# Second SwiGLU half step of a hybrid decoder layer: gate and up products by seven block products instead of eight

## The chip, the cores and the metric

The kernel runs on one core of a Trainium2 chip. Its engines are named as the profile names them: PE (matrix products, with PEld for the loads of its stationary operand), DVE (elementwise, VectorE), ACT (activations and copies, ScalarE), POOL (elementwise, GpSimd) and SP, which issues the DMAs. The metric is the device time of one execution in microseconds; a kernel is given by the median of its runs. Before the change it is 2705.25 us over 3 runs (2701.61 to 2705.65).

## The reference

One layer of a decoder trunk over 1056 tokens (1024 of a prompt, 32 sample tokens; 16 more tokens only in the first part), with D_MODEL 1024 and D_FF 2816, all in float32:

```python
def _swiglu(x, w_gate, w_up, w_down):
    return (jax.nn.silu(x @ w_gate) * (x @ w_up)) @ w_down

h = h + 0.5 * _swiglu(_rmsnorm(h, norm_ffn1), ffn1_w_gate, ffn1_w_up, ffn1_w_down)
z = _rmsnorm(h, norm_mix) @ w_in            # gated linear attention and S5 branches follow
merged = jax.nn.sigmoid(gate_a) * gla_out + jax.nn.sigmoid(gate_b) * s5_out
h = h + merged @ w_out
h = h + 0.5 * _swiglu(_rmsnorm(h, norm_ffn2), ffn2_w_gate, ffn2_w_up, ffn2_w_down)
return _rmsnorm(h, norm_final)
```

The change concerns the last three lines: the output projection, the second half step and the final norm.

## The kernel before

Activations lie transposed, features on the 128 partitions and tokens along the free axis, so a matrix with 1024 rows is 8 tiles of 128 by 1024. The 1056 tokens are cut in chunks `CH2` of 256, 384 and 416 columns. Each operand of a large product is held as two float32r parts, a rounded one and a rest (`xh`, `xl` of the activations, `wh`, `wl` of the weights), and each product is three matmuls: `wh` with `xh`, `wh` with `xl`, `wl` with `xh` (L702 to L704 in `group`). A job of 8 row tiles is 24 matmuls into one PSUM buffer of the pool `mm` (4 buffers).

The class `Weights` streams weight tiles of 128 x 1024 in the order of use: SP loads one (512 KB), ACT copies it to `wh` (L598), DVE subtracts to `wl` (L610), two tiles ahead of PE. `tiles` runs a list of jobs over the chunks; after each job `sch.slot()` lets background work go a step further. The program order of each engine is the order in which this code is written out; an engine executes its list in that order.

The output projection (`w_out`, from L1503) has 8 weight tiles and goes in two passes: 8 tiles over chunks 0 and 1, then the same 8 tiles over chunk 2. After each job DVE adds the PSUM to `h` (L36), ACT squares the result and POOL adds the square to a running sum (`nacc`, L36). When a chunk is complete, `sums` makes column sums on PE (L796) and a reciprocal root by 13 small DVE operations (`rq`); `apply` spreads it by PE (L814) and makes the normalized chunk: DVE multiplies from PSUM (`at`, L52), ACT rounds (`xh`, L692), DVE and POOL in turn subtract (`xl`, L693).

The second half step (`ffn`, L851) works through the 22 tiles of D_FF in groups of 2, 4, 4, 4, 4, 4. In a group each tile has a gate job and an up job for each chunk (72 matmuls each over the three chunks), then come the down jobs of the group, added to `h` by DVE (L52). The first group starts with three jobs on chunks 0 and 1, so that chunk 2 can be normalized beside them. The last group's down jobs go chunk by chunk, with the final norm behind each.

## Time and profile before

| what | value |
|---|---|
| median of 3 runs | 2705.25 us |
| profiled execution, own time | 2706.03 us |
| its span, first to last instruction | 2704.3 us |
| mean granted PE clock | 0.993 |
| busy PE / DVE / ACT / POOL | 98% / 46% / 26% / 18% |
| output projection, second pass | about 1894 to 1931 us |
| second half step, first gate job to last down job | about 1937 to 2693 us |

A line of the groups view gives the source line, engine, operation, output and inputs by their names, then the number of instructions, busy time and mean duration. Matmuls are pipelined: the duration of one (0.28 to 0.35 us) is longer than the distance from one start to the next, and it is the distance that counts. In a row of the timeline the first number is the start in us from the beginning of the span, the second the time from there to the end of the last of the merged instructions.

### The profile page before, as it was taken

How to read it: one execution, taken by the hardware profiler on the slowest of the kernel's cores; microseconds unless marked ns; L12 is line 12 of the kernel's file. 1: busy time of each engine (PE TensorE's matmuls, PEld its weight loads, DVE VectorE, ACT ScalarE, POOL GpSimd, SP SyncE). 2: the span in 40 equal slices, each digit the busy share in tenths (PEclk: the TensorE clock that was granted, in tenths of full speed). 3: DMA queues.
4: the chain of work that ended last, by engine and by line, in shares of the span. 5: the costliest groups of instructions: out<-in, count | busy, mean ns of one | idle time of the engine just before them, and what ended most of it. 6: DMA issues, size and time to landing. Idle time of an engine off the chain costs nothing. (4 is left out here: it accounts for less than half of the span.)

```text
span 2704.3 us, 41257 instructions
## 1 busy us (share of the span) xinstructions
PE 2654.9 (98%) x16796; PEld 2602.6 (96%) x16796; DVE 1237.9 (46%) x2677; ACT 713.8 (26%) x1303; POOL 479.1 (18%) x1006
## 2 busy tenths in 40 slices
...
GB/s 122 47 47 40 47 48 50 133 138 99 62 26 192 191 198 201 137 51 55 83 79 52 146 108 195 116 157 81 71 47 48 47 47 41 46 47 48 47 47 65
DMA packets 135790, 236.92 MB, mean 88 GB/s; under 512 B 21872, under 2 KB 100016, under 8 KB 134576
## 3 DMA queue, kind: packets, MB, share of 16 engines
...
## 5 line engine op out<-in xcount | busy, mean ns | idle before, releaser
L702 PE MATMUL mm<-xh,wh 128*128 128x256 f32 (+3 forms) x3648 | 1193.8, 327 | 19.6 <-ACT ta L1051 10.9
L704 PE MATMUL mm<-xh,wl 128*128 128x256 f32 (+3 forms) x3648 | 1186.3, 325 | 3.1 <-DVE wl L610 3.1
L703 PE MATMUL mm<-xl,wh 128*128 128x256 f32 (+3 forms) x3648 | 1184.1, 325 | 0.7 <-POOL xl L693 0.5
L702 PEld LDWEIGHTS mm<-xh,wh 128*128 128x128 f32 x3648 | 693.3, 190 | 30.6 <-ACT ta L1051 11.1
L704 PEld LDWEIGHTS mm<-xh,wl 128*128 128x128 f32 x3648 | 692.7, 190 | 8.9 <-DVE wl L610 4.0
L703 PEld LDWEIGHTS mm<-xl,wh 128*128 128x128 f32 x3648 | 693.3, 190 | 8.2 <-POOL xl L693 1.6
L610 DVE TENSOR_TENSOR wl<-wr,wh 128x1024 fp32r<-128x1024 f32 x218 | 270.4, 1240 | 347.4 <-ACT wh L598 346.7
L598 ACT ACTIVATE wh<-wr 128x1024 fp32r<-128x1024 f32 x218 | 229.0, 1052 | 483.8 <-PE mm L703 368.1
L702 PE MATMUL mm<-ah,wh 128*128 128x256 f32 (+3 forms) x1008 | 326.2, 324 | 0.6 <-DVE h L52 0.3
L703 PE MATMUL mm<-al,wh 128*128 128x256 f32 (+3 forms) x1008 | 326.3, 324 | 0.0
L704 PE MATMUL mm<-ah,wl 128*128 128x256 f32 (+3 forms) x1008 | 325.1, 323 | 0.0
L36 POOL TENSOR_TENSOR nacc<-nacc,nsq 128x384 f32<-128x384 f32 (+3 forms) x63 | 65.0, 1032 | 1049.0 <-ACT nsq L778 1044.7
L702 PEld LDWEIGHTS mm<-ah,wh 128*128 128x128 f32 x1008 | 189.4, 188 | 3.1 <-DVE h L52 0.7
L704 PEld LDWEIGHTS mm<-ah,wl 128*128 128x128 f32 x1008 | 189.5, 188 | 1.4
L703 PEld LDWEIGHTS mm<-al,wh 128*128 128x128 f32 x1008 | 189.3, 188 | 1.3
L692 ACT ACTIVATE ah<-at 128x256 fp32r<-128x256 f32 x132 | 66.1, 501 | 410.1 <-DVE at L36 410.1
L36 DVE TENSOR_TENSOR at<-mm,sg 128x256 f32<-128x256 f32 x132 | 69.3, 525 | 210.1 <-PE mm L704 199.2
L52 DVE SCALAR_TENSOR_TENSOR g<-mm,g 128x256 f32<-128x256 f32 (+2 forms) x144 | 74.5, 523 | 128.1 <-PE mm L704 127.6
L36 POOL TENSOR_TENSOR sg<-sg,root 128x384 f32<-128x384 f32 (+1 forms) x44 | 47.4, 1079 | 474.9 <-ACT sg L866 474.8
L52 DVE SCALAR_TENSOR_TENSOR h<-mm,h 128x256 f32<-128x256 f32 (+2 forms) x144 | 74.4, 526 | 74.0 <-PE mm L704 73.2
L693 DVE TENSOR_TENSOR al<-at,ah 128x256 fp32r<-128x256 f32 x132 | 70.4, 533 | 74.8 <-ACT ah L692 74.8
L49 POOL TENSOR_SCALAR rq<-rq,rq 128x1 f32<-128x1 f32 (+1 forms) x216 | 86.4, 400 | 21.7
...
## 6 DMA issues: line engine op xcount, KB each, us to landing
...
```

What stands on the lines that cost most here:

```text
L36: (eng or self.nc.vector).tensor_tensor(out=out, in0=a, in1=b, op=op)
L49: (eng or self.nc.vector).tensor_scalar(out=out, in0=a, scalar1=s1, scalar2=s2, op0=op0, **kw)
L52: self.nc.vector.scalar_tensor_tensor(out=out, in0=a, scalar=s, in1=b, op0=op0, op1=op1)
L598: self.nc.scalar.activation(out=h, in_=r, func=AF.Copy)
L610: e.tensor_tensor(out=l, in0=r, in1=h.bitcast(FT), op=OP.subtract)
L692: act.activation(out=xh, in_=t, func=AF.Copy)
L693: (eng or v).tensor_tensor(out=xl, in0=t, in1=xh.bitcast(FT), op=OP.subtract)
L702: pe.matmul(p, wh[:, b], xh, start=(k == 0), stop=False)
L703: pe.matmul(p, wh[:, b], xl, start=False, stop=False)
L704: pe.matmul(p, wl[:, b], xh, start=False, stop=(k == nk - 1))
```

## The change

Two adjacent tiles of D_FF, the two halves of the 1024 features and two halves of a block of tokens form a 2 x 2 by 2 x 2 block product. Before it was eight block products. Now it is seven, of sums and differences of blocks (Strassen's scheme in Winograd's form). One such set for gate or for up of two tiles is a `unit`: 7 products of 4 row tiles and 3 matmuls, 84 matmuls for each token block. There are two token blocks: block 0 with halves of 330 columns, block 1 with halves of 198. 11 pairs of tiles make 22 units.

- Sums of activations: seven operands a block, each in two float32r parts (`V[p][i]`), made once. For block 0 `early0` makes two of them beside the second pass of the output projection, and `late0` the other five beside the third. For block 1 `all1` makes them beside the first units: for each of 4 pairs of feature tiles, spread over 8 jobs, DVE makes 4 normalized blocks and 4 rests, POOL 4 differences and 3 rests, ACT 7 roundings.
- Sums of weights: the class `Stream` loads quarters of 128 x 512, makes four sums a unit on POOL, and rounds and subtracts each of seven on ACT and DVE (128 x 512 each), two products ahead (`LEAD = 2`).
- Outputs: three PSUM banks `a`, `b`, `c` a block; the order is `abcaaca`, so four products go into `a`. ACT copies partial sums out (`copy`), DVE adds them (`out`).
- The output projection has chunks of 264, 396 and 396 columns (`CHM`) and three passes, chunk 2, chunk 0, chunk 1, so 24 weight tiles instead of 16. `h` is one tile `H`, loaded after the projection before it.
- The first pairs (gate and up of pair 0, gate of pair 1, down of pair 0) run on block 0 alone and then on block 1 alone. From then on both blocks run within a product. The down jobs have widths 352 (or 330 and 396 for a single block), and the last two pairs go together, in four chunks of 330, 330, 198, 198 with the final norm behind each.
- Small edits elsewhere: scratch tiles shared in the S5 set-up, one load moved there, three instead of four buffers for the root.

```diff
+CHM = [(0, 264), (264, 396), (660, 396)]
...
+    HN, HP = (330, 198), (0, 660)
...
+    def nrm(p, k, i, R, t=None):
+        q0 = HP[p] + i * HN[p]
...
+        o.stt(t, H[:, k, q0:q0 + HN[p]], par[:, 24 + k:25 + k], R, OP.mult, OP.mult)
+        return t
+    def hi_(p, i, kp, t):
+        act.activation(out=V[p][i][0][:, kp], in_=t, func=AF.Copy)
+    def lo_(p, i, kp, t, eng):
+        xh, xl = V[p][i]
+        o.sub(xl[:, kp], t, xh[:, kp].bitcast(FT), eng)
...
+    def late0(R0, R):
+        roots(0, 1, R)
+        yield
+        x = {}
+        def a(kp):
+            x12, x22 = nrm(0, kp, 1, R), nrm(0, kp + 4, 1, R)
+            t1 = nrm(0, kp, 0, R0, tq.tile([P, HN[0]], FT, name="t1", bufs=2))
+            o.sub(t1, x12, t1)
+            hi_(0, IT1, kp, t1)
+            hi_(0, I22, kp, x22)
+            o.sub(x12, x22, x12, g)
+            x[kp] = [x12, x22, t1]
+        def b(kp):
+            x12, x22, t1 = x[kp]
+            lo_(0, IT1, kp, t1, v)
+            lo_(0, I22, kp, x22, v)
+            o.sub(x22, x22, t1)
+            hi_(0, IT3, kp, x12)
+            hi_(0, IT2, kp, x22)
+            t4 = nrm(0, kp + 4, 0, R0, tq.tile([P, HN[0]], FT, name="t4", bufs=2))
+            o.sub(t4, t4, x22, g)
+            x[kp].append(t4)
+        def c(kp):
+            x12, x22, t1, t4 = x.pop(kp)
+            lo_(0, IT3, kp, x12, g)
+            lo_(0, IT2, kp, x22, v)
+            hi_(0, IT4, kp, t4)
+            lo_(0, IT4, kp, t4, g)
+        for s in range(6):
+            for d, f in enumerate((c, b, a)):
+                kp = s - 2 + d
+                if 0 <= kp < 4:
+                    f(kp)
+            yield
+    def all1(R):
...
+    AB, A_, B_ = (0, 1), (0,), (1,)
+    plan = [(k, n, ps_) for ps_ in (A_, B_) for k, n in (("g", 0), ("u", 0), ("g", 1), ("d", 0))]
+    for n in range(1, NP - 1):
+        plan += [("u", n, AB), ("g", n + 1, AB)] + ([("d", n, AB)] if n < NP - 2 else [])
+    plan += [("u", NP - 1, AB), ("e", NP - 2, AB)]
...
+    class Stream:
+        LEAD = 2
...
+            T.append(((x, 0), lambda: a11, ()))
+            T.append((None, s3, ()))
+            T.append(((x, 1), lambda: a12, ()))
+            T.append((None, lambda: (o.add(a21, a21, a22, g), o.sub(a11, a22, r[0], g)), ()))
+            T.append(((x, 2), lambda: a21, (2,)))
+            T.append(((x, 3), lambda: a11, ()))
+            T.append((None, lambda: o.sub(a12, a12, a11, g), ()))
+            T.append(((x, 4), lambda: r[0], (0,)))
+            T.append(((x, 5), lambda: a12, (1,)))
+            T.append(((x, 6), lambda: a22, (3,)))
...
-    for m in range(8):
-        for c in range(2):
-            w_out(m, c, wi + m)
-    n3.fin(0, 1)
-    n3.fin(1, 3)
     for m in range(8):
         w_out(m, 2, wi + 8 + m)
-    n3.fin(2, 3)
...
+    sch.later(1, lambda: n3.sums(2))
+    sch.later(2, lambda: sch.add(early0(R0)))
     for m in range(8):
+        w_out(m, 0, wi + 8 + m)
...
+    sch.later(1, lambda: n3.sums(0))
+    sch.later(2, lambda: sch.add(late0(R0, SGs[0][:, 0])))
+    for m in range(8):
+        w_out(m, 1, wi + 16 + m)
+        if m == 6:
+            ws = Stream()
+    n3.sums(1)
+    sch.drain()
...
+    ws.advance(0)
+    ws.flush()
...
+    BANK = "abcaaca"
...
+        for i in range(7):
+            b = ws.get((x, i), num[0])
...
+            for p in ps_:
...
+                ps = bank[p, BANK[i]]
+                xh, xl = V[p][i]
+                for k in range(4):
+                    wh, wl = b[:, P * k:P * k + P], b[:, 512 + P * k:512 + P * k + P]
+                    pe.matmul(ps, wh, xh[:, k], start=FIRST[i] and k == 0, stop=False, skip_group_check=True)
+                    pe.matmul(ps, wh, xl[:, k], start=False, stop=False, skip_group_check=True)
+                    pe.matmul(ps, wl, xh[:, k], start=False, stop=(k == 3), skip_group_check=True)
```

DVE in the last pass of the output projection, from one addition to `h` (L36, out of `mm`) to the next; first before, then after. In both, `wl` is the rest of the next weights; after, `e1`, `e3`, `e5` are rests of operands and `t`, `t1`, `t4` normalized blocks or their sums.

```order
L36 TENSOR_TENSOR g2_18499<-mm_19252,g2_18499 128x416
L52 SCALAR_TENSOR_TENSOR at_19282<-g1_16624,par_65,sm_19227 128x384
L52 SCALAR_TENSOR_TENSOR at_19286<-g1_16624,par_65,sm_19227 128x384
L693 TENSOR_TENSOR xl1_19232<-at_19282,xh1_19231 128x384
L52 SCALAR_TENSOR_TENSOR at_19290<-g1_16624,par_65,sm_19227 128x384
L52 SCALAR_TENSOR_TENSOR at_19294<-g1_16624,par_65,sm_19227 128x384
L693 TENSOR_TENSOR xl1_19232<-at_19290,xh1_19231 128x384
L610 TENSOR_TENSOR wl_19301<-wr_19196,wh_19300 128x1024
L36 TENSOR_TENSOR g2_18499<-mm_19305,g2_18499 128x416
```

```order
L36 TENSOR_TENSOR h2_18493<-mm_19320,h2_18493 128x396
L36 TENSOR_TENSOR e3_19120<-t_19257,e2_19119 128x330
L36 TENSOR_TENSOR e1_19118<-t1_19311,e0_19117 128x330
L36 TENSOR_TENSOR e5_19122<-t_19309,e4_19121 128x330
L36 TENSOR_TENSOR t_19309<-t_19309,t1_19311 128x330
L52 SCALAR_TENSOR_TENSOR t4_19358<-h2_18493,par_65,r0_18783 128x330
L52 SCALAR_TENSOR_TENSOR t_19361<-h2_18493,par_65,xh0_19115 128x330
L52 SCALAR_TENSOR_TENSOR t_19363<-h2_18493,par_65,xh0_19115 128x330
L52 SCALAR_TENSOR_TENSOR t1_19365<-h2_18493,par_65,r0_18783 128x330
L36 TENSOR_TENSOR t1_19365<-t_19361,t1_19365 128x330
L617 TENSOR_TENSOR wl_19372<-wr_19268,wh_19371 128x1024
L36 TENSOR_TENSOR h2_18493<-mm_19374,h2_18493 128x396
```

Between the two additions six operations on 384 columns became nine on 330, and the root that the multiplications read is no longer in PSUM (`sm`) but in SBUF (`r0`, `xh0`).

POOL in the same pass, first before and then after, to the end of the pass and the first weight sum (`s3`). `nacc` and `f0` are the running sums of squares, `xl1`, `e7`, `e8` rests of operands.

```order
L36 TENSOR_TENSOR nacc0_19042<-nacc0_19042,nsq_19225 128x416
L693 TENSOR_TENSOR xl1_19232<-at_19243,xh1_19231 128x384
L693 TENSOR_TENSOR xl1_19232<-at_19286,xh1_19231 128x384
L693 TENSOR_TENSOR xl1_19232<-at_19294,xh1_19231 128x384
L36 TENSOR_TENSOR nacc0_19042<-nacc0_19042,nsq_19280 128x416
```

```order
L36 TENSOR_TENSOR f0_19158<-f0_19158,f2_18506 128x396
L36 TENSOR_TENSOR e7_19124<-t_19361,e6_19123 128x330
L36 TENSOR_TENSOR e8_19125<-t4_19412,xl0_19116 128x330
L36 TENSOR_TENSOR t4_19462<-t4_19462,t_19417 128x330
L36 TENSOR_TENSOR f0_19158<-f0_19158,f2_18506 128x396
L36 TENSOR_TENSOR e7_19124<-t_19415,e6_19123 128x330
L36 TENSOR_TENSOR e8_19125<-t4_19462,xl0_19116 128x330
L36 TENSOR_TENSOR f0_19158<-f0_19158,f2_18506 128x396
L36 TENSOR_TENSOR s3_19544<-wr_19465,wr_19466 128x512
```

The last sum of squares now stands behind the last operands of block 0, and the first weight sum behind that.

PE at the end of the last pass, before and after: the last matmul of the output projection and what follows.

```order
L704 MATMUL mm_19375<-xh2_17623,wl_19301 128x416
L702 MATMUL mm_19410<-xh0_19102,wh_19335 128x256
L703 MATMUL mm_19410<-xl0_19103,wh_19335 128x256
L704 MATMUL mm_19410<-xh0_19102,wl_19336 128x256
L702 MATMUL mm_19410<-xh0_19102,wh_19335 128x256
```

```order
L715 MATMUL mm_19471<-xh1_17614,wl_19372 128x396
L809 MATMUL sm_19504<-one1_68,f0_19158 128x1 x4
L1890 MATMUL mm_19542<-xh2_18781,wv_19534 128x330
L1891 MATMUL mm_19542<-xh2_18781,wv_19534 128x330
L1892 MATMUL mm_19542<-xh2_18781,wv_19534 128x330
```

Before, a gate job on a chunk that was long normalized followed at once; now the column sums of the chunk just finished stand in front of the first product.

## Rows read from the trace of the kernel before

**Rows 1.** The page, busy time of PE and its loads, share, instructions.
```profile
PE 2654.9 (98%) x16796; PEld 2602.6 (96%) x16796; DVE 1237.9 (46%) x2677; ACT 713.8 (26%) x1303; POOL 479.1 (18%) x1006
```
**Rows 2.** Windows: length, then busy PE, PEld, DVE, ACT, POOL, granted clock, DMA.
```profile
1993.57:2086.10 92.53, 92.53 (x578) 92.19 (x576) 21.82 (x31) 18.69 (x31) 0.00 (x0) 1.00 0.14 46
2086.10:2131.98 45.88, 45.88 (x289) 45.72 (x288) 17.64 (x29) 4.68 (x5) 0.00 (x0) 1.00 0.14 47
...
1916.30:1920.30 4.00, 4.00 (x13) 3.87 (x14) 2.25 (x3) 1.50 (x2) 1.94 (x2) 0.57 0.37 131
```
**Rows 3.** Timeline of PE, gate and up jobs, 256 and then 384 columns.
```profile
2051.40 0.28 PE L702 MATMUL mm<-xh,wh 128*128 128x256 f32 x1
...
2052.95 0.28 PE L703 MATMUL mm<-xl,wh 128*128 128x256 f32 x1
...
2055.31 0.33 PE L702 MATMUL mm<-xh,wh 128*128 128x384 f32 x1
...
2056.35 0.33 PE L702 MATMUL mm<-xh,wh 128*128 128x384 f32 x1
```
**Rows 4.** Timeline of PEld around the one-column sums of squares.
```profile
1894.49 0.53 PEld L796 LDWEIGHTS sm<-one,nacc 128*128 128x128 f32 x4
1894.94 0.19 PEld L702 LDWEIGHTS mm<-xh,wh 128*128 128x128 f32 x1
```
**Rows 5.** Timeline of PE, second pass of the output projection; in brackets idle time and releaser.
```profile
1913.67 0.35 PE L704 MATMUL mm<-xh,wl 128*128 128x416 f32 x1
1915.02 0.45 PE L702 MATMUL mm<-xh,wh 128*128 128x416 f32 x1 [1.00 <-ACT wh L598]
1915.32 0.35 PE L703 MATMUL mm<-xl,wh 128*128 128x416 f32 x1
1916.28 0.45 PE L704 MATMUL mm<-xh,wl 128*128 128x416 f32 x1 [0.61 <-DVE wl L610]
```
**Rows 6.** Groups by form from 1600 us on, DVE and POOL on SBUF operands.
```profile
L610 DVE TENSOR_TENSOR wl<-wr,wh 128x1024 fp32r<-128x1024 f32 x98 | 120.4, 1228 | 245.3 <-ACT wh L598 245.3
...
L693 DVE TENSOR_TENSOR al<-at,ah 128x384 fp32r<-128x384 f32 x22 | 12.3, 559 | 13.0 <-ACT ah L692 13.0
...
L693 DVE TENSOR_TENSOR al<-at,ah 128x256 fp32r<-128x256 f32 x22 | 9.4, 426 | 10.6 <-ACT ah L692 10.6
...
L36 POOL TENSOR_TENSOR nacc<-nacc,nsq 128x384 f32<-128x384 f32 x14 | 14.2, 1016 | 35.0 <-ACT nsq L778 35.0
L36 POOL TENSOR_TENSOR nacc<-nacc,nsq 128x256 f32<-128x256 f32 x7 | 5.2, 737 | 273.5 <-ACT nsq L778 273.5
```
**Rows 7.** Timeline of POOL, then of DVE, second pass of the output projection.
```profile
1905.73 1.02 POOL L693 TENSOR_TENSOR xl<-at,xh 128x384 fp32r<-128x384 f32 x1 [3.56 <-ACT xh L692]
1906.70 1.09 POOL L36 TENSOR_TENSOR nacc<-nacc,nsq 128x416 f32<-128x416 f32 x1
...
1915.06 2.11 POOL L36 TENSOR_TENSOR nacc<-nacc,nsq 128x416 f32<-128x416 f32 x1
...
1906.83 1.38 DVE L693 TENSOR_TENSOR xl<-at,xh 128x384 fp32r<-128x384 f32 x1
1908.13 1.21 DVE L610 TENSOR_TENSOR wl<-wr,wh 128x1024 fp32r<-128x1024 f32 x1
1909.27 0.58 DVE L36 TENSOR_TENSOR g<-mm,g 128x416 f32<-128x416 f32 x1
...
1915.00 1.23 DVE L610 TENSOR_TENSOR wl<-wr,wh 128x1024 fp32r<-128x1024 f32 x1 [0.91 <-ACT wh L598]
1916.14 0.58 DVE L36 TENSOR_TENSOR g<-mm,g 128x416 f32<-128x416 f32 x1
```
**Rows 8.** Waits of PE from 1600 us on: total, times, longest.
```profile
PE sm L814 <- DVE rq L52: 2.5, 1, 2.5
```
**Rows 9.** Groups by form from 1600 us on, ACT reading PSUM.
```profile
L862 ACT ACTIVATE sg<-mm 128x384 f32<-128x384 f32 x22 | 10.8, 490 | 80.9 <-PE mm L704 80.9
...
L862 ACT ACTIVATE sg<-mm 128x256 f32<-128x256 f32 x22 | 8.4, 384 | 23.3 <-PE mm L704 23.3
```

More of the change, by code (lines that the diff above doesn't have):

```diff
@@ L593, in split_to @@
     def split_to(self, n):
-        while self.ns <= min(n, len(self.order) - 1):
+        while self.ns <= min(n, self.end - 1):
             self.load_to(self.ns)
@@ new lines, in build, with roots @@
+    sqs = e_(2, 1, FT)
+    n3 = Norm(tp, CHM, h, 24, acc=lambda c, i: e_((1, 0, 0)[c], int(c != 2), FT), sq=sq_)
+    V = {}
+    I11, I21, IT1, IT2, IT3, I22, IT4 = range(7)
+    def roots(p, i, out):
+        q0, n = HP[p] + i * HN[p], HN[p]
+        r = ps_sm()[:, :n]
+        x = 0
+        while x < n:
+            c = max((c for c in range(3) if COLS[c] <= q0 + x), key=lambda c: COLS[c])
+            t = q0 + x - COLS[c]
+            cuts, rs = n3.rs[c]
+            j = max(j for j, u in enumerate(cuts) if u <= t)
+            a = t - cuts[j]
+            w = min(P - a, n - x)
+            pe.matmul(r[:, x:x + w], rs[:, j:j + 1].to_broadcast([P, P]), ident[:, a:a + w], start=True, stop=True)
+            x += w
+        act.activation(out=out, in_=r, func=AF.Copy)
@@ new lines, in build @@
+    pairs, i0 = [], A["order"][-n_ffn]
+    for gi, fs in enumerate(FGROUPS):
+        for a in range(0, len(fs), 2):
+            pairs.append((gi, a, i0 + 2 * a, i0 + 2 * len(fs)))
+        i0 += 3 * len(fs)
+    NP = len(pairs)
+    AB, A_, B_ = (0, 1), (0,), (1,)
[3 more added lines that the diff above has]
+    plan += [("u", NP - 1, AB), ("e", NP - 2, AB)]
@@ L1507, in w_out @@
         sch.slot()
+    TB = 8
+    ctq = ExitStack()
+    tq = pool(ctq, "f2q", side="right")
     for m in range(8):
[L1509 to L1518 removed]
+        w_out(m, 2, wi + m)
+    xf = {f"x{i}2": xa.tile([P, 2 * 1320 + 792], FR, name=f"x{i}2") for i in "hl"}
@@ new lines, in build @@
+    x0 = xa.tile([P, 4 * HN[0] + 4 * HN[1]], FR, name="xl0")
+    for j, i in enumerate((IT1, IT2, I22, IT3)):
+        V[0][i] = tuple(q4(e_(2 * j + q, 0)) for q in range(2))
+    V[0][IT4] = part(x0, 0, 0), q4(e_(8, 0))
+    sch.later(1, lambda: n3.sums(0))
[6 more added lines that the diff above has]
+    sch.drain()
+    wi += 24
+    ctq.close()
+    wctx.close()
@@ new lines, in build, with tt_, rest, a_home @@
+    fw = pool(ch2, "f2w")
+    fa = pool(ch2, "f2a")
+    ws.advance(0)
+    ws.flush()
+    num = [0]
+    BANK = "abcaaca"
+    FIRST = (True, True, True, False, False, False, False)
+    aH, lq, parity = {}, [], [0]
+    def tt_(p):
+        return tp.tile([P, HN[0]], FT, name="t", bufs=TB)[:, :HN[p]]
+    def rest():
+        for l, t, hh in lq:
+            o.sub(l, t, hh.bitcast(FT))
+        del lq[:]
+    def a_home(n, p, f, i):
+        if n == NP - 1:
+            return [V[p][I11][z][:, 2 * f + i] for z in range(2)]
+        q = HP[p] + HN[p] * i
+        return [aH[n][f][z][:, q:q + HN[p]] for z in range(2)]
@@ new lines, in cols, with down @@
+    def cols(n, t0, nn):
+        return [[y[:, t0:t0 + nn] for y in aH[n][f]] for f in range(2)]
+    def down(x, n, ps_):
+        rest()
+        for q in range(4):
+            b = ws.get((x, q), num[0])
+            num[0] += 1
+            for j in range(2):
+                m = 2 * q + j
+                for t0, nn in CHD[ps_]:
+                    ps = down_group([b], j, t0, nn, [cols(n, t0, nn)])
+                    o.stt(H[:, m, t0:t0 + nn], ps, 0.5, H[:, m, t0:t0 + nn], OP.mult, OP.add)
+                    ws.flush()
+                    sch.slot()
```

313 lines of the change are left out of this document (277 added, 36 removed).

## The prediction, made before the result was known

> **What bounds the kernel now.** I read the page's busy shares first: PE is busy for 98% of the span [rows 1]. A pipelined engine can look busy without being full, so next came the windows of one group of the second half step: 576 gate and up matmuls in 92.53 us, 288 down matmuls in 45.88 us, the granted clock 1.00, POOL idle, DVE busy for a quarter of it [rows 2]. That is 0.1606 and 0.1593 us a matmul. In the timeline the start-to-start distance is 1.55/13 = 0.119 us at 256 columns and 1.04/6 = 0.173 us at 384 [rows 3], so a matmul costs about 0.4 ns a column plus a fixed part. PE is full here; only fewer or shorter matmuls can save time, and every wait put in front of PE is lost in full. The place where DVE and POOL are late already is the second pass of the output projection [rows 5].
>
> **The change part by part.** The sum is made against the profiled execution, 2706.0 us (span 2704.3), 0.8 us above the median of 2705.25.
>
> *Gate and up.* Before: 22 tiles x 144 = 3168 matmuls x 0.1606 = 508.9 us. After: 22 units x 84 = 1848 at 330 columns and 1848 at 198. For 330 the line between the two distances gives 0.150 us. 198 columns is narrower than any matmul of this kind in the trace. Lower bound: the same line further down, 0.119 - 58 x 0.42 ns = 0.095. Upper bound: no shorter than at 256, 0.120. A third row is nearer than either: four loads of a full 128 x 128 stationary tile, with matmuls of one column between them, start 0.45/4 = 0.112 us apart [rows 4]. Each of our matmuls needs its own load, so the load is the floor. I take 0.112. After: 1848 x (0.150 + 0.112) = 484.2, that is -24.7 us (-56 at 0.095, -10 at 0.120).
> The Trainium skill, "TensorE: Matmul & The Clock Gate", section "LDWEIGHTS (loading the stationary operand)", puts a load at the number of its columns divided by 1.2 GHz, 107 ns for 128. The trace's 112 ns agrees within 5; by the page's figure the sum would be some 10 us lower (2040 narrow matmuls).
>
> *Down.* A pair of tiles takes 144 matmuls, 22.9 us. Nine pairs keep 1056 columns in other widths: 0.06 us more each, +0.5. The last two take 96 x (2 x 0.150 + 2 x 0.112) = 50.3 instead of 45.9: +4.4. Together +5. The stream of PE so saves 20 us.
>
> *Output projection.* The same number of matmuls over 264 + 396 + 396 columns: no change. Eight more weight tiles (1.2 us of DVE each) lie beside groups of 3 to 4.3 us: nothing, where DVE is free. It is not free in the third pass.
>
> *Operands beside the third pass.* What DVE and POOL do there must be added up together, since the trace shows that they do not run together on SBUF operands. POOL's `nacc` started at 1906.70 and ran 1.09 us; DVE's `xl`, started at 1906.83, took 1.38 us instead of the 0.56 of its like, to the end of POOL's operation and 0.4 us more. Conversely `nacc`, started at 1915.06 behind DVE's `wl` (1915.00, 1.23 us), took 2.11 us. DVE's addition out of PSUM at 1916.14 ran at its 0.58 us beside POOL [rows 6, 7]. So DVE operations with two SBUF inputs and POOL operations make one queue, and nearly all that `late0` adds is of these kinds: the root too is now in SBUF.
> The Trainium skill, "SBUF — State Buffer", section "Who interferes with whom", says the same: the port pair that DVE and GpSimd share is an exclusive lock, and the later one blocks fully. By that rule the operands cost what I add up now; without it they would fit beside PE, a rival below. The rows above agree with it.
> Prices, less the 0.08 (DVE) or 0.05 us (POOL) by which neighbours overlap [rows 6, 7]: at 330 columns DVE 0.42, POOL 0.85; `wl` 1.14; a `nacc` of 396 columns 1.0. From the end of the pass's third group five groups remain, 5 x 24 x 0.178 (396 columns on the same line) = 21.4 us. In that time stand 4 x 9 DVE operations (15.1), 4 x 4 POOL operations (13.6), 3 `wl` (3.4), 6 `nacc` (6): 38 us, 17 more than there is. Behind the queue's last piece, the last `nacc`, come the column sums, the root chain (PE waited 2.5 us for it at the end of before [rows 8]) and the rest of the first new weights (512 columns, 0.6): 3.4 more. PE's first product stands behind all of this. A walk through the queues in program order, with ACT's copies of the weights for the groups 7 and 8 standing behind the copies of operands, gives 26 us. Between 20 and 26 I take 23, in part ahead of the last two groups. Had the two engines run side by side, DVE alone would need 21.4 us and the end chain would leave 5.5: the lower bound.
> After a wait of some 2 us in the second pass of before, the clock fell to its lower level (1.2 GHz): 13 matmuls in 4 us at a mean granted clock of 0.57 [rows 2, 5]; that cost 1.6 us. I count 2 after the wait. Before's own waits there, 1.2 + 0.8 + 1.6 = 3.5, go. Sum: +21.5.
>
> *First units, one block at a time.* A unit on block 0 alone takes PE 84 x 0.150 = 12.6 us. In it the shared queue holds seven rests of weights (512 columns, 0.60: 4.2), four weight sums on POOL (2.2 ns a column from 256 to 384, so 1.25: 5.0) and 7/8 of a step of `all1` (8 DVE operations of 0.285, 7 on POOL of 0.56, at 198 columns: 5.4): 14.6; for up also 7 of 0.42: 17.5. Three units: 46.7 against 37.9 of PE. +9. On block 1 alone: 9.2 and 11.2 against 84 x 0.112 = 9.4: +2. In these units product 5 goes into bank `a` directly behind product 4, whose copy by ACT (0.33 to 0.44 us [rows 9]) it waits for, with the drain 0.5 to 0.6: six times, of which the three on block 0 lie within the 9. +2.
>
> *Units on both blocks.* The queue needs 4.2 + 5.0 + 7 x 0.705 = 14.1 us for up, PE 22.0; weights have two products of 3.1 us. Hidden. If the cover were gone, each microsecond missing would come 19 times.
>
> *The rest.* The set-up edits and the load moved lie beside full PE: nothing. `H` is now loaded after the gating projection; its first 1.6 MB must land within the first group's 4.3 us and four PSUM buffers behind it: nothing, up to 5. The end has a last chunk of 198 instead of 256 columns: -0.5.
>
> Sum: -20 + 21.5 + 9 + 2 + 2 - 0.5 = +14, from 2706.0 to 2720; less 0.8, on the footing of the median, 2719. I take 2720.
>
> **The rivals.** *A: the narrow matmul follows its columns* (0.095). For it: the line of rows 3 has no break down to 256. Against it: rows 4. PE saves 54 instead of 20; the units on block 1 then are bound by the shared queue (8.0 against 9.2 and 11.2), +3. 2720 - 31 = 2689, faster.
> The Trainium skill, "TensorE: Matmul & The Clock Gate", section "Back-to-back issue gap", gives a lone matmul columns over 2.4 GHz plus 2.5 ns, 85 ns here, which would take off 20 more; it names the load as a second limit, as rows 4 show it.
> *B: operands hidden as the schedule means it.* For it: DVE and POOL are busy for 46 and 18% of the span [rows 1]. Against it: rows 7. Then 5.5 + 2 - 3.5 = 4 for the passage and nothing for the units on block 0: -20 + 4 + 2 + 2 - 0.5 = -13, 2692, faster.
> *C: half of the queueing lies in slack that my walk misses* (POOL's pieces fall beside DVE's PSUM reads and its waits for ACT): 11 instead of 23, 4 instead of 9, so 2703, no change.
> *D: both go badly:* 0.120 a narrow matmul (+16), 28 at the passage (+5), 14 for the units on block 0 (+5), 5 for `H`: 2750. It decides where the load needs the fixed part of rows 3 on top.
>
> **How the numbers follow.** Forecast 2708 to 2740, chance 0.46; D and beyond 0.15; C 0.13; A 0.13; B 0.13. Times within 0.2% (5.4 us) are what a measurement of this kernel cannot tell from no change. Slower: 0.46 + 0.15 and a little of C: 0.62. Same: 0.12. Faster: 0.26. The range 2691 to 2746 leaves out about 0.1 on each side; the likeliest case alone has 2708 to 2740.
>
> **What would show it.** Right: PE starts at 198 columns 0.11 us apart; a wait of PE of 15 us or more in all in the last two groups of the output projection and before the first product, its releasers DVE `wl`, ACT `wh`, DVE `rq` and POOL's sum of squares; DVE operations there stretched beside POOL; a unit on both blocks at 22 us without waits. Wrong: narrow matmuls at 0.10 us or below, a passage under 8 us, or repeated waits for weights in the later units, which I priced at nothing.

## The result, and the profile after

The changed kernel takes 2754.47 us (median of 4 runs, 2753.86 to 2758.39); before takes 2705.45 (2701.61 to 2706.53). The ratio is 1.0187, 95% interval 1.0175 to 1.0199: slower by 49 us, where 14 were forecast, and outside the range of 2691 to 2746. The profiled execution took 2753.9 us (span 2752.1 against 2704.3, +47.8).

First the busy line of the page and then the stages of the second half step as windows of after. Columns: the stretch and its length, busy PE, PEld, DVE, ACT, POOL, then the granted clock, DMA share, GB/s. In order: the three passes of the output projection (the last with the wait for its column sums), the sums with the first product, the rest of the units on block 0, the units on block 1, two units on both blocks, and a projection down. The column sums of a pass stand behind the first group of the next one, so a window of a pass ends with that group.

```profile
PE 2666.3 (97%) x17434; PEld 2609.2 (95%) x17434; DVE 1465.8 (53%) x3187; ACT 848.4 (31%) x1688; POOL 649.4 (24%) x1149
```

```profile
1824.34:1867.10 42.76, 39.45 (x218) 38.72 (x217) 16.52 (x20) 13.47 (x18) 7.27 (x7) 0.96 0.59 200
1867.10:1902.38 35.28, 29.63 (x208) 27.91 (x206) 21.95 (x41) 15.05 (x25) 8.41 (x11) 0.95 0.34 109
1902.38:1951.60 49.22, 35.63 (x183) 34.11 (x183) 35.74 (x63) 18.56 (x37) 24.75 (x24) 0.86 0.21 73
1951.60:1961.54 9.94, 7.38 (x30) 6.96 (x31) 5.17 (x16) 1.41 (x3) 5.69 (x4) 0.51 0.09 26
1961.54:2010.10 48.56, 40.72 (x243) 38.01 (x242) 34.20 (x56) 25.19 (x57) 22.42 (x24) 0.96 0.19 60
2025.75:2067.44 41.69, 35.69 (x254) 33.55 (x253) 23.39 (x41) 18.16 (x41) 17.11 (x12) 0.88 0.23 73
2076.10:2120.42 44.32, 44.32 (x337) 44.32 (x337) 23.06 (x44) 18.06 (x41) 10.10 (x7) 1.00 0.17 54
2120.42:2143.53 23.11, 23.11 (x146) 23.11 (x145) 14.10 (x27) 2.75 (x5) 5.38 (x4) 1.00 0.12 35
```

Against [rows 1] PE is busy for as large a share and for 11 us longer, so its share tells nothing of the loss; DVE has 228 us more, POOL 170. The last two windows answer to [rows 2] and are close to what was forecast: two units take 44.32 us without a wait, 22.16 each, where 22.0 were forecast. The new stalls all lie in the 252 us ahead of them. (In PE's timeline of before, the second pass of the output projection lies at 1880 to 1922 us and the first gate job starts at 1922; the table ahead of the prediction has these times 9 to 15 us too late.)

The seven largest groups of waits of PE in after, from 1700 us on: total, times, longest. They answer to [rows 5, 8].

```profile
PE sm L809 <- POOL f L36: 9.8, 2, 9.2
PE mm L713 <- ACT wh L605: 8.1, 4, 3.7
PE mm L1892 <- DVE wv L36: 7.8, 9, 2.6
PE mm L1890 <- ACT t L1879: 5.3, 6, 2.2
PE mm L715 <- DVE wl L617: 4.6, 7, 1.2
PE mm L1890 <- ACT wv L1768: 3.1, 4, 1.1
PE sm L827 <- DVE rq L52: 2.5, 1, 2.5
```

The last stood in before as well; the others are spread over six releasers, and no single wait is the cause. The waits in the 252 us come to 39 us, which is less than the loss counted below: for the rest of it PE is busy, but slower. The granted clock of the six windows with stalls is 0.51 to 0.96, lowest in the window of the first product, behind the wait of 9.2 us.

For the account, each stage of after is set beside its matmuls at the full-clock distances that the timeline shows (198 columns 0.112 us, 264 0.122, 330 0.152, 396 0.180) plus its column sums and root broadcasts (0.11 us each or less). The other columns are runs below. Lengths in us, from the first matmul of a stage to that of the next:

| stage | matmuls alone | after | e1 | e2 | e3 | e6 | e7 | e12 | e8 | e11 |
|---|---|---|---|---|---|---|---|---|---|---|
| first pass | 37.5 | 42.8 | 43.5 | 43.5 | 42.5 | 37.5 | 42.4 | 44.1 | 37.5 | 37.5 |
| second pass | 26.3 | 35.3 | 26.8 | 36.6 | 28.8 | 35.3 | 35.3 | 35.3 | 27.9 | 28.1 |
| third pass, wait for its sums | 31.8 | 49.2 | 34.7 | 50.6 | 50.8 | 49.3 | 49.2 | 44.7 | 45.8 | 51.3 |
| sums, first product, roots | 3.7 | 9.9 | 10.1 | 9.2 | 9.1 | 10.1 | 9.8 | 9.1 | 9.5 | 4.7 |
| units on block 0 | 36.5 | 48.6 | 40.6 | 43.0 | 47.2 | 48.4 | 42.4 | 47.1 | 40.4 | 35.4 |
| down, block 0 | 14.6 | 15.7 | 14.5 | 17.0 | 15.7 | 15.7 | 16.1 | 15.7 | 19.6 | 18.0 |
| units on block 1 | 28.2 | 41.7 | 37.9 | 33.3 | 40.6 | 40.0 | 34.2 | 39.2 | 33.5 | 34.7 |

(e8 and e11 have blocks of other widths: there the matmuls alone are 29.3 us for the fifth row, 11.7 for the sixth and 30.7 for the last. In e11 the sums stand behind the first two products, which so count in the third row, and the third product in the fourth; its fifth row has two products less than the others', 26.4 us of matmuls.)

After's stalls and low clock add up to 5.3 + 9.0 + 17.4 + 6.2 + 12.1 + 1.1 + 13.5 = 65 us. I had counted 23 + 2 + 9 + 2 + 2 = 38.

### The profile page after: what moved, and what is told of

The parts are those of the page before. It is cut to its first block, busy times and chain, and to the rows that moved or that the text cites. A ratio compares the mean times of both kernels' runs of the same rounds, so it can differ in the third digit from the quotient of the medians.

```text
span 2752.1 us, 44143 instructions
## 1 busy us (share of the span) xinstructions
PE 2666.3 (97%) x17434; PEld 2609.2 (95%) x17434; DVE 1465.8 (53%) x3187; ACT 848.4 (31%) x1688; POOL 649.4 (24%) x1149
## 3 DMA queue, kind: packets, MB, share of 16 engines
q1 hardware_dynamic: 155840, 242.68, 27.9%
## 4 chain that ended last, share of the span: by engine, by line
PE 87%; DVE 4%; ACT 2%; DMA 1%; POOL 1%; issue 1%; SPq 0%; POOLq 0%; ACTq 0%; DVEq 0%
PE mm L713 18%; PE mm L714 17%; PE mm L715 17%; PE mm L1892 5%; PE mm L1890 5%; PE mm L1891 5%; PE mm L1918 3%; PE mm L1920 3%; PE mm L1919 3%; PE mm L1348 1%; PE mm L1349 1%; PE mm L1350 1%; PE sm L1891 1%; PE sm L1890 1%; PE sm L1892 1%
## 5 line engine op out<-in xcount | busy, mean ns | idle before, releaser
L713 PE MATMUL mm<-xh,wh 128*128 128x256 f32 (+5 forms) x2592 | 855.8, 330 | 25.4 <-ACT ta L1064 10.8
L715 PE MATMUL mm<-xh,wl 128*128 128x256 f32 (+5 forms) x2592 | 847.4, 327 | 7.1 <-DVE wl L617 7.1
L714 PE MATMUL mm<-xl,wh 128*128 128x256 f32 (+5 forms) x2592 | 849.0, 328 | 0.6 <-POOL xl L704 0.5
L713 PEld LDWEIGHTS mm<-xh,wh 128*128 128x128 f32 x2592 | 494.2, 191 | 36.3 <-ACT ta L1064 11.0
L715 PEld LDWEIGHTS mm<-xh,wl 128*128 128x128 f32 x2592 | 494.0, 191 | 14.2 <-DVE wl L617 9.9
L714 PEld LDWEIGHTS mm<-xl,wh 128*128 128x128 f32 x2592 | 494.4, 191 | 7.0 <-POOL xl L704 1.6
L52 DVE SCALAR_TENSOR_TENSOR h<-mm,h 128x352 f32<-128x352 f32 (+6 forms) x392 | 200.4, 516 | 173.4 <-PE mm L1920 98.8
L36 DVE TENSOR_TENSOR wv<-wr,wv 128x512 fp32r<-128x512 f32 x190 | 142.5, 751 | 65.1 <-ACT wv L1768 64.9
L714 PE MATMUL mm<-al,wh 128*128 128x256 f32 (+2 forms) x504 | 164.1, 326 | 0.0
L36 POOL TENSOR_TENSOR sg<-sg,root 128x384 f32<-128x384 f32 (+1 forms) x44 | 47.9, 1090 | 463.8 <-ACT sg L879 463.8
L1918 PE MATMUL mm<-ah,wv 128*128 128x352 f32 (+2 forms) x432 | 139.6, 323 | 0.6 <-DVE h L52 0.6
L1920 PE MATMUL mm<-ah,wv 128*128 128x352 f32 (+2 forms) x432 | 139.2, 322 | 0.0
L1891 PE MATMUL mm<-e,wv 128*128 128x330 f32 x440 | 138.8, 315 | 0.0
L36 POOL TENSOR_TENSOR wr<-wr 128x512 f32<-128x512 f32 x50 | 72.3, 1446 | 209.1 <-DMA wr<-wst 122.6
L1890 PE MATMUL mm<-e,wv 128*128 128x330 f32 x352 | 113.7, 323 | 4.9 <-ACT t L1879 4.1
L1892 PE MATMUL mm<-e,wv 128*128 128x330 f32 x352 | 112.0, 318 | 1.4 <-DVE wv L36 1.4
```

What stands on the lines that cost most here:

```text
L36: (eng or self.nc.vector).tensor_tensor(out=out, in0=a, in1=b, op=op)
L52: self.nc.vector.scalar_tensor_tensor(out=out, in0=a, scalar=s, in1=b, op0=op0, op1=op1)
L713: pe.matmul(p, wh[:, b], xh, start=(k == 0), stop=False)
L714: pe.matmul(p, wh[:, b], xl, start=False, stop=False)
L715: pe.matmul(p, wl[:, b], xh, start=False, stop=(k == nk - 1))
L1890: pe.matmul(ps, wh, xh[:, k], start=FIRST[i] and k == 0, stop=False, skip_group_check=True)
```

## The experiments

Each run's ratio is to the kernel before. Upstream of the change the same instructions end up to 5.6 us apart from run to run (the gating projection starts between 1730.3 and 1735.9 us in the profiles), so a difference of 2 or 3 us is read from the stages and not from a median.

**e1: no operands.**

```diff
-                t = nrm(0, kp + z, 0, R)
-                hi_(0, i, kp, t)
-                lo_(0, i, kp, t, g if z else v)
+                if z == 0:
+                    hi_(0, i, kp, H[:, kp, 0:HN[0]])
...
+    V0, V[0] = V[0], [(V[0][I11][0],) * 2] * 7
...
+            V[1] = [(V[1][I11][0],) * 2] * 7
```

> Left out: the making of the operands in early0, late0 and all1 (all their products, sums and low parts); only the high part of one block is copied by ACT, and all seven products read it for both parts. PE has the same matmuls. Theory Q (the queues of DVE, ACT and POOL, which carry the operands, hold PE up in the last two passes of the output projection, before the first product and in the units on one block): the second pass loses 10 of its 13 us, the third 13 of 14, the wait for POOL's sum of squares 7 of 9.6, the units on block 0 11 of 16.6, those on block 1 9 of 13.5: some 45 to 50 us, 2705 to 2710. Rival W (it is the weights: loads that queue behind H, their splits and sums): the passes and units keep their length, a gain of at most 15, 2740 or more.

2719.63 us, ratio 1.0064 (1.0048 to 1.0079): 35 us come back, between the two, nearer to Q. Without any operand work the kernel is still slower than before. The table shows where nothing came back: the units on block 1 still take 37.9 instead of 28.2, so most of their loss has nothing to do with operands, and the first pass is as in after. The second pass is nearly whole again (26.8 us, where its matmuls need 26.3), although its eight additional weight tiles are still there; the third comes back to 34.7.

**e2: all on DVE.**

```diff
-                lo_(0, i, kp, t, g if z else v)
+                lo_(0, i, kp, t, v)
...
-            o.sub(x12, x22, x12, g)
+            o.sub(x12, x22, x12, v)
...
-                o.sub(r[0], a11, a21, g)
+                o.sub(r[0], a11, a21, v)
```

So every `g` in `late0`, `all1` and `Stream.unit`, and `n3` with `engs=(v,)`.

> All that POOL does between the output projection and the end (subtractions of late0, low parts, sums of weight blocks, sums of squares of n3) goes to DVE: at 330 columns 0.42 instead of 0.85 us each, and nothing is left to exclude. Theory L (exclusion, one queue for both engines): the passage has some 14 us less work in that queue and the units on block 0 some 3 each: 8 to 20 us faster, 2735 to 2746. Rival R (what binds is each engine's own queue, worked off in order, DVE waiting for ACT and ACT for DVE; POOL beside it is mostly free help): DVE's queue grows by about 1.7 us a group in the third pass and by 3 us a unit: 5 to 15 us slower, 2760 to 2770.

2748.29 us, 1.0167 (1.0151 to 1.0182): faster by 6, where L said 8 to 20 and R said slower. The gain is all in the units on one block (14 us); the second pass is 1.3 us longer, and the third, which L should have helped most, is no shorter. Its rows show why both theories hold half. Windows of the third pass, columns as above: e2, and e12 (below).

```profile
1907.79:1958.40 50.61, 36.04 (x183) 34.24 (x183) 38.81 (x84) 18.28 (x36) 0.00 (x0) 0.88 0.19 63
```

```profile
1903.08:1947.82 44.74, 36.12 (x182) 34.27 (x182) 33.47 (x63) 18.36 (x37) 8.09 (x8) 0.90 0.24 80
```

Without POOL, DVE does 84 operations in 38.8 us; in after it did 63 in 35.7, with POOL busy for 24.8 beside it. The exclusion is real: the same two products of `late0`, in the timeline of DVE first in after beside POOL's 1.15 us operation and then in e2 (start, length):

```profile
1939.01 1.66 DVE L52 SCALAR_TENSOR_TENSOR t<-h,par,xh 128x330 f32<-128x330 f32 x2
```

```profile
1939.16 1.15 POOL L36 TENSOR_TENSOR t<-t,t 128x330 f32<-128x330 f32 x1 [0.91 <-DVE t L52]
```

```profile
1948.43 1.03 DVE L52 SCALAR_TENSOR_TENSOR t<-h,par,xh 128x330 f32<-128x330 f32 x2
```

But what DVE gains by being alone (0.46 us an operation instead of 0.57) it spends on the 21 operations of POOL's share.

**e12: late0 without POOL.**

```diff
-            o.sub(x12, x22, x12, g)
-            o.sub(t4, t4, x22, g)
-            lo_(0, IT3, kp, x12, g)
-            lo_(0, IT4, kp, t4, g)
...
+                if p == 0 and i in (IT3, IT4):
+                    xl = xh
```

> Left out: the sixteen operations of late0 on POOL (two differences and two low parts of each step; the products 4 and 6 of block 0 then read a high part for both). DVE, ACT and PE have the same instructions; the sums of squares stay on POOL. It tells whether POOL's work beside the third pass costs time. Theory L (DVE and POOL exclude each other on SBUF operands): DVE's operations shrink from a mean of 0.56 us to some 0.47 in the third pass and POOL's last sum of squares comes early: the pass, with the wait for it, loses 8 to 11 us, 2743.5 to 2746.5. Rival R (DVE's own queue, in order and waiting for ACT, is what is late): only the last sum of squares comes earlier, 2 to 4 us, 2750.5 to 2752.5.

2748.94 us, 1.0167 (1.0150 to 1.0184): 5.5 us, again between. The third pass keeps 13 of its 17 us of loss: POOL's sixteen operations cost some 4.5. What keeps the rest shows in one round, from one addition to `h` to the next. In after it goes from 1926.51 to 1935.72, 9.2 us, where PE needs 24 x 0.180 = 4.3; DVE is busy for 7.2 of them. In e12 it still takes 8.5, with DVE busy for 6.6. The end of the round in after, DVE and then ACT (start, length; in brackets the idle time before it and who ended it):

```profile
1934.58 1.23 DVE L617 TENSOR_TENSOR wl<-wr,wh 128x1024 fp32r<-128x1024 f32 x1 [1.86 <-ACT wh L605]
1935.72 0.56 DVE L36 TENSOR_TENSOR h<-mm,h 128x396 f32<-128x396 f32 x1
```

```profile
1932.76 0.85 ACT L1573 ACTIVATE e<-t 128x330 fp32r<-128x330 f32 x2 [2.58 <-DVE t L36]
1933.51 1.04 ACT L605 ACTIVATE wh<-wr 128x1024 fp32r<-128x1024 f32 x1
```

ACT's copy of the weights stands behind two copies of operands, the first of which DVE has only just made; DVE waits for the weights' copy, and the next addition stands behind its rest. In the whole pass DVE's waits for these copies add up (total, times, longest):

```profile
DVE wl L617 <- ACT wh L605: 9.1, 5, 1.9
```

So DVE's own work in a round is longer than PE's, and to it comes a wait of up to 1.9 us. Whether another order of `late0` would take that wait away was not tested.

**e3: early0 in stages.**

```diff
-        for kp in range(4):
-            for i, z in ((I11, 0), (I21, 4)):
-                t = nrm(0, kp + z, 0, R)
-                hi_(0, i, kp, t)
-                lo_(0, i, kp, t, g if z else v)
+        x = {}
+        for s in range(6):
+            if s >= 2:
+                for i, z in ((I11, 0), (I21, 4)):
+                    lo_(0, i, s - 2, x.pop((s - 2, z)), g if z else v)
+            if 1 <= s < 5:
+                for i, z in ((I11, 0), (I21, 4)):
+                    hi_(0, i, s - 1, x[s - 1, z])
+            if s < 4:
+                for z in (0, 4):
+                    x[s, z] = nrm(0, s + z, 0, R)
```

> early0 in three stages, each a group later: multiply by the root, copy by ACT, low part. The same operations; DVE no longer waits for ACT inside a group, and the weight copy of ACT no longer stands behind a copy whose input was just made. Theory R (a ring of DVE and ACT, each in order: addition, product, copy, low part, product, copy, weight copy, weight rest = 5.5 us a group): about 4.5 us a group remain, 5 to 7 us faster, 2747 to 2749. Rival L (exclusion of DVE and POOL): the same work in the same queue, within 2 us of 2754.5. Rival W (arrival of weights): nothing.

2748.06 us, 1.0172 (1.0155 to 1.0189): R. The second pass falls from 35.3 to 28.8 with the same operations. One round of the ring in after, the timeline of DVE, then of ACT, and what POOL did at its end (start, length, engine, line, tiles; in brackets the idle time before it and who ended it):

```profile
1875.18 0.42 DVE L36 TENSOR_TENSOR h<-mm,h 128x264 f32<-128x264 f32 x1
1875.52 0.55 DVE L52 SCALAR_TENSOR_TENSOR t<-h,par,r 128x330 f32<-128x330 f32 x1
1876.62 0.50 DVE L36 TENSOR_TENSOR xh<-t,xh 128x330 fp32r<-128x330 f32 x1 [0.55 <-ACT xh L1573]
1877.05 0.56 DVE L52 SCALAR_TENSOR_TENSOR t<-h,par,r 128x330 f32<-128x330 f32 x1
1879.10 1.79 DVE L617 TENSOR_TENSOR wl<-wr,wh 128x1024 fp32r<-128x1024 f32 x1 [1.50 <-ACT wh L605]
1880.81 0.42 DVE L36 TENSOR_TENSOR h<-mm,h 128x264 f32<-128x264 f32 x1
```

```profile
1875.70 0.43 ACT L791 ACTIVATE f<-h 128x264 f32<-128x264 f32 x1 [1.69 <-DVE h L36]
1876.11 0.48 ACT L1573 ACTIVATE xh<-t 128x330 fp32r<-128x330 f32 x1
1877.63 0.48 ACT L1573 ACTIVATE xl<-t 128x330 fp32r<-128x330 f32 x1 [1.04 <-DVE t L52]
1878.02 1.04 ACT L605 ACTIVATE wh<-wr 128x1024 fp32r<-128x1024 f32 x1
```

```profile
1879.05 0.75 POOL L36 TENSOR_TENSOR f<-f,f 128x264 f32<-128x264 f32 x1
```

From one addition to the next 5.63 us pass, where PE needs 24 x 0.122 = 2.9. DVE's low part waits for ACT's copy; ACT's second copy waits for DVE's second product; the weight copy stands behind it; the weight rest waits for that, and beside POOL it takes 1.79 instead of 1.23; and the next addition stands behind the rest. Both engines are idle for a good part of it (of 5.6 us DVE works 3.6 and ACT 2.3): neither is full, they take turns.

**e4: equal halves.**

```diff
-    HN, HP = (330, 198), (0, 660)
+    HN, HP = (264, 264), (0, 528)
...
-    CHD = {AB: [(0, 352), (352, 352), (704, 352)], A_: [(0, 330), (330, 330)], B_: [(660, 396)]}
+    CHD = {AB: [(0, 352), (352, 352), (704, 352)], A_: [(0, 264), (264, 264)], B_: [(528, 264), (792, 264)]}
...
```

The tiles that hold the operands are laid out anew for these widths.

> Both blocks are 2 x 264 columns instead of 2 x 330 and 2 x 198. Theory F (a matmul of 198 columns is bound by the load of its stationary tile, 0.112 us, so its columns are not worth less than some 230): a unit on both blocks takes 84 x 2 x 0.122 = 20.5 us instead of 22.17, nineteen of them give 32, the last products down 4, the units on one block together 0 to 5: 2714 to 2719. Rival C (time goes with columns, the sum of which is the same): 2752 to 2757, units on both blocks at 22 us.

2717.99 us, 1.0058 (1.0043 to 1.0073): F, at its figure. Two units on both blocks, in this run's window:

```profile
2073.44:2114.28 40.84, 40.84 (x339) 40.84 (x338) 23.28 (x46) 18.14 (x41) 6.69 (x5) 1.00 0.19 59
```

20.42 us a unit instead of 22.16 with the same columns in all; over nineteen units that is 33 us of the 36.5. Narrow matmuls meet a floor: those of 1, 128 and 198 columns start 0.112, 0.111 and 0.112 us apart, those of 264 already 0.122. Each of them has its own load of a 128 x 128 tile, so the load is the likely floor; no run varied it. By the line of [rows 3] 198 columns would take 0.095, so some 0.02 of their 0.112 buy nothing (an estimate). The third pass, too, is 4.1 us shorter in e4 (45.1), and most other stages changed a little.

**e5: another order of the products.**

```diff
-            T.append((None, lambda: (o.add(a21, a21, a22, g), o.sub(a11, a22, r[0], g)), ()))
-            T.append(((x, 2), lambda: a21, (2,)))
+            T.append((None, lambda: (o.sub(a11, a22, r[0], g), o.add(a21, a21, a22, g)), ()))
             T.append(((x, 3), lambda: a11, ()))
+            T.append(((x, 2), lambda: a21, (2,)))
...
-        for i in range(7):
+        for i in (0, 1, 3, 2, 4, 5, 6):
```

> The seven products in the order 0, 1, 3, 2, 4, 5, 6, so that no product goes into bank a directly behind another one that goes there (a b a c a c a). Theory B (PE waits for ACT's copy out of the bank between products 3 and 4 of each unit on one block): six waits, 5.3 us in the trace, go: 4 to 6 us faster, 2749 to 2751. Rival W (the weights of product 4 or 5 are late as well): the wait comes back under the name of a weight, less than 1.5 us gained, 2753 to 2755.

2747.82 us, 1.0163 (1.0148 to 1.0178): 6.7 us, slightly more than B said. The units on block 0 fall from 48.6 to 43.7 us; their window, to be set beside the fifth of after:

```profile
1961.44:2005.15 43.71, 39.12 (x242) 36.59 (x243) 34.39 (x56) 24.88 (x57) 22.42 (x23) 1.00 0.22 69
```

PE is idle for 4.6 us instead of 7.8 and keeps its full clock. The waits of PE for a copy, in the windows of the units: in after on block 0 and on block 1, and then the same in e5 (total, times, longest):

```profile
PE mm L1890 <- ACT t L1879: 4.1, 3, 2.2
PE mm L1890 <- ACT t L1879: 1.3, 3, 0.4
```

```profile
PE mm L1890 <- ACT t L1879: 2.0, 3, 1.2
PE mm L1890 <- ACT t L1879: 3.0, 3, 1.1
```

They did not go, as B has it: on block 0 they halved, on block 1 they grew, and in all they are nearly as long as in after (5.0 against 5.3 us). What went besides is the wait for copies of weights (3.1 us in after). The edit also has POOL make the sums in the other order, so how much of the gain is the bank's and how much the weights' stays open.

**e6: H later.**

```diff
-            nc.sync.dma_start(H[:, k0:k1, COLS[c]:COLS[c] + n], hsp[:, k0:k1, t0:t0 + n])
+            if c == 2:
+                nc.sync.dma_start(H[:, k0:k1, COLS[c]:COLS[c] + n], hsp[:, k0:k1, t0:t0 + n])
...
         w_out(m, 2, wi + m)
+        if m in (2, 3, 4, 5, 6, 7):
+            c, k0 = (0, 0, 0, 1, 1, 1)[m - 2], (0, 3, 6)[(m - 2) % 3]
+            k1, (t0, n) = min(k0 + 3, 8), CHM[c]
+            nc.sync.dma_start(H[:, k0:k1, COLS[c]:COLS[c] + n], hsp[:, k0:k1, t0:t0 + n])
```

> The loads of H for the second and third pass are issued in pieces behind the groups 3 to 8 of the first pass instead of all six ahead of it. Theory Q (the wait of 3.0 us in the first pass is for weights queued behind 4.3 MB of H): that wait goes, and the half clock behind it: 3 to 4.5 us faster, 2750 to 2751.5. Rival C (the later loads delay the weights of the passes they now lie in): no gain or 1 to 3 us slower, 2754 to 2757.

The first pass goes from 42.8 to 37.5 us, without a wait and at full clock: Q. First ACT's wait for the weights in after, then the window of the pass in e6:

```profile
1843.39 1.06 ACT L605 ACTIVATE wh<-wr 128x1024 fp32r<-128x1024 f32 x1 [8.47 <-DMA wr<-wst]
```

```profile
1827.69:1865.24 37.55, 37.55 (x217) 37.47 (x216) 16.73 (x20) 13.48 (x18) 7.27 (x7) 1.00 0.66 225
```

The median falls only to 2752.64, 1.0181 (1.0165 to 1.0196), between Q and C. The profiled execution of e6 started the pass 3.3 us later than after's did, upstream of the edit; whether the others did so too is not known.

**e7: weight sums on DVE.**

```diff
-                o.sub(r[0], a11, a21, g)
+                o.sub(r[0], a11, a21, v)
...
-            T.append((None, lambda: (o.add(a21, a21, a22, g), o.sub(a11, a22, r[0], g)), ()))
+            T.append((None, lambda: (o.add(a21, a21, a22, v), o.sub(a11, a22, r[0], v)), ()))
...
-            T.append((None, lambda: o.sub(a12, a12, a11, g), ()))
+            T.append((None, lambda: o.sub(a12, a12, a11, v), ()))
```

> The four sums of weight blocks of each unit go from POOL (1.27 us each, two or three in a row) to DVE (0.69); everything else stays on POOL. Theory P (a chain, not a sum: product 2 waits until POOL has done the first difference and the sum behind it, 2.5 us from the arrival of the blocks, while products 0 and 1 last 2.7 us on block 1): units on block 1 lose 7 to 9 us of 13.5, on block 0 4 to 6 of 16.6: 11 to 15 us faster, 2740 to 2744; units on both blocks stay at 22.17. Rival S (weights arrive late from DMA): within 2 us of 2754.5. Rival D (DVE's queue, worked off in order, gets longer and the sums wait in it behind operands): 0 to 5 us slower.

2742.47 us, 1.0147 (1.0132 to 1.0162), 12.0 us faster: P. The units on block 1 fall from 41.7 to 34.2, on block 0 from 48.6 to 42.4, those on both blocks stay. The chain in after, at the head of a unit on block 1, timelines of POOL, ACT and PE:

```profile
2055.89 1.85 POOL L36 TENSOR_TENSOR wr<-wr 128x512 f32<-128x512 f32 x1 [6.60 <-DMA wr<-wst]
2057.70 1.27 POOL L36 TENSOR_TENSOR wr<-wr,s 128x512 f32<-128x512 f32 x1
```

```profile
2057.77 0.63 ACT L1768 ACTIVATE wv<-wr 128x512 fp32r<-128x512 f32 x1 [1.37 <-POOL wr L36]
```

```profile
2058.46 0.36 PE L1890 MATMUL mm<-xl,wv 128*128 128x198 f32 x1 [0.25 <-ACT wv L1768]
2059.58 0.36 PE L1892 MATMUL mm<-xl,wv 128*128 128x198 f32 x1 [0.65 <-DVE wv L36]
```

POOL had been idle for 6.6 us until a block came. Then its sum (1.85 us beside DVE, 1.27 alone), ACT's copy and DVE's rest (1.09 us beside POOL, 0.68 alone) follow one another, and PE waits at the end of the row; the second sum is what product 3 waits for. In the three units on block 1 product 2 takes 2.3, 3.3 and 2.3 us in after, where its twelve matmuls need 1.34, and in the second of them the products 3 to 5 then take 3.2, 2.7 and 2.4 with only one short wait among them. In e7 product 2 takes 1.9 in each. DVE's sums are shorter than POOL's and no longer stretch the rests; which of the two counts more is not separated, and when a block arrives was not varied: 6.0 of the 13.5 us on block 1 stay. In e7 the window of these units has no POOL, and the clock stays at 1.00:

```profile
2020.69:2054.85 34.16, 30.98 (x252) 29.09 (x253) 26.16 (x52) 17.93 (x41) 0.00 (x0) 1.00 0.29 89
```

**e9: the last sums later** (on after).

```diff
-    n3.sums(1)
     sch.drain()
...
         if x == 0:
+            def go():
...
+                sch.add(all1(SGs[1]))
+            sch.later(2, lambda: n3.sums(1))
+            sch.later(3, go)
```

> The column sums and root of the last chunk (needed for block 1 alone) are issued behind the second product of the first unit instead of ahead of the first product; nothing else is changed. Theory O (the 9.2 us that PE waits for POOL's sum of squares is a matter of order: the first products need nothing of it, and their operands are ready some 4 us before it): 6 to 9 us faster, 2745 to 2748. Rival L (late0's own operands are late: the wait comes back at the third product, behind DVE or POOL): 0 to 3 us, 2751 to 2755.

2756.32 us, 1.0189 (1.0175 to 1.0203): nothing gained, so neither as O nor quite as L said. The wait came back at the first product, not the third (waits of PE, 1950 to 1966 us, and ACT in front of that product):

```profile
PE mm L1889 <- ACT wv L1768: 6.7, 1, 6.7
PE sm L809 <- POOL f L36: 1.3, 1, 1.3
```

```profile
1948.99 0.48 ACT L1573 ACTIVATE e<-t 128x330 fp32r<-128x330 f32 x1 [2.76 <-DVE t L36]
1950.83 1.13 ACT L1768 ACTIVATE wv<-wr 128x512 fp32r<-128x512 f32 x2
```

ACT's copies of the first weights stand behind its last copies for `late0`, and those behind DVE. The 9.2 us were never POOL's sum of squares alone: the queues of DVE and ACT were late as well. `all1` now starts later, and the units on block 1 took 46.7.

**e8, e11: what helped, together.** e8 has e3, e4, e5, e6 and e7; e11 has e9 as well.

> All that helped or should: equal blocks of 264 columns, early0 in three stages, order of products 0, 1, 3, 2, 4, 5, 6, the H loads spread, weight sums on DVE. If the gains add: 36.5 (measured) + 6.4 (measured) + 5 + 4 + 13 = 65, 2690: faster than before by 15. If they cover each other (waits in a row, the later hidden by the earlier; POOL's sum of squares of 9 us stays): 2700 to 2710, no better than before.

> e8_combined with the column sums of the last chunk behind the second product. Theory O: the wait of 7.2 us shrinks by 5 to 7: 2688 to 2691, 0.5 to 0.6% faster than before. Rival L: within 2 us of 2695.4.

e8: 2695.42 us, 0.9968 (0.9958 to 0.9979). That is 59 of the 65 us, nearer to gains that add. e11: 2688.99, 0.9943 (0.9931 to 0.9956), faster than both kernels, before by 15 us. Here the later column sums do pay, by the size that O gave, but not by its way: the wait of 7.2 us for POOL went and one of 4.8 us for the first weights came, and the third and fourth rows of the table together come to 56.0 instead of 55.3 us, with two products (2.9 us) more in them. As much of the gain lies in the units on block 0, which have these two less and take 35.4 instead of 40.4. Which of the five edits makes the difference to e9 was not tested.

**e10: the limit.** e1 with e4, e5, e6 and e7.

> Left out: the making of the operands, as in e1_no_operands; with equal blocks, the order 0, 1, 3, 2, 4, 5, 6, the H loads spread and the weight sums on DVE. It tells how much all further work on the operands could give at most. If the gains measured one by one add: 2719.6 - 36.5 - 6.7 - 1.8 - 12 = 2663. If weights and operands held the same units up (one hidden by the other), 2672 to 2680.

2665.93 us, 0.9857 (0.9842 to 0.9872): nearly the 2663 of gains that add. e11 is 23 us longer; that is about what another arrangement of the operands could still give in this structure. It is no strict bound, since e10 still makes some of the copies and has its column sums in front of the first product. By the profiles some 15 of the 23 lie between the second pass and the end of the units on block 0, and 6 in the down of block 0, which takes 18.0 us in e11 and 11.6 in e10.

## Why the prediction was wrong

*Right.* The direction, and this much of the mechanism: operands beside the passes cost more than the stream saves (35 us by e1 against some 14). The narrow matmul at 0.112 us: rival A falls. Later units without waits. The third pass with the first product: 25 us gross were forecast, 17.4 + 6.2 = 23.6 came, and rivals B and C fall by that. PE's waits in the third pass and for its sums add up to 14.1 us, where 15 were named as a sign.

That this number came out is in part luck, for its reason was only half right. That DVE and POOL make one queue holds for the operations that meet (e2). The Trainium skill, "SBUF — State Buffer", section "Who interferes with whom", calls the port pair that the two share an exclusive lock. The two products that took 1.66 us beside POOL and 1.03 without it agree. But my sum had POOL's sixteen operations at 13.6 us, and without them 4.5 came back (e12), three quarters of the pass's loss staying. Beside DVE's own work stand its waits for ACT's copies of weights, 9.1 us in the pass, which the sum of 38 us did not hold (the walk behind it had them for two groups).

*The stream*, -20.5 with the end forecast, came out near -14 (what is left of the 47.8 when the stages, before's own 3.5 us of waits and 0.7 us upstream are taken off): the 330 columns took 0.152 instead of 0.150 (3 us over 19 units), down 1, the end 1.5, and the last 1 is not traced.

*Failed: nothing for the second pass.* "Eight more weight tiles (1.2 us of DVE each) lie beside groups of 3 to 4.3 us: nothing, where DVE is free. It is not free in the third pass." The tiles do cost nothing where DVE is free (e1), but `early0` had no term at all, and the pass lost 9.0 us. I compared each engine's busy time with PE's and looked for lateness in the third pass only; `early0` I never walked. DVE was free in the sum and late in the order: e3 gives 6.5 of the 9.0 back by order alone.

*Failed: "`H` ... nothing, up to 5."* It cost slightly more than the upper bound, 5.3. Not H's first piece was late, as I had checked, but the weights queued behind its later 2.6 MB (e6): ACT waited 8.5 us for them.

*Failed: "On block 1 alone ... +2".* It cost 13.5 with the bank's share. My sum of the shared queue, 9.2 to 11.2 us against 9.4, was an average over the unit. What binds is a chain at its head: the last block arrives, then POOL's sums, a copy, a rest (e7, which alone gives 7.5 back; e1 shows that operands are a minor part). Nor had I a term for the clock there: of the 13.5 us PE is idle for 6.0, for the rest it is busy at a granted clock of 0.88. On block 0, where I had +9, it was +12; e1, e5 and e7 each take 5 to 8 us of that away, so their causes overlap and are not separated.

These terms, 5.3 + 9.0 + 9.5 more than counted, and 4 on block 0, less 1.4 too many at the third pass, make the 26.6 us of missed stalls; the stream's 6.5 and the 0.7 upstream are the rest of the 33.8 by which the spans missed the forecast.

Rival D had 2750, but mostly by another way: it put the excess into matmuls of 0.120, the third pass, block 0 and `H`. Of these `H` came, and on block 0 3 of its 5 us.
